# Attention scores by head, w_ada in pieces of 256 rows, and more buffers for the first shift and scale, in a two-block network on one core

## The chip, the cores and the metric

One Trainium2 chip, one core of it. The metric is the device time of one execution in microseconds. Before: 2873.4 us, the median of 3 runs (2872.57 to 2875.65).

## The reference

`reference()` runs two transformer blocks on 256 tokens of width 2048, in fp32. The first block has two layers, and the change lies in these. Cut to what matters:

```python
mod = c_act @ w_ada[l] + b_ada[l]                  # one row of 2048 by [2048, 6144]
shift, scale, gate = jnp.split(mod, 3, axis=-1)
h = rms_norm(x, norm_g[l]) * (1.0 + scale[:, None, :]) + shift[:, None, :]
u, z_s, q, k, v, z_a = jnp.split(h @ w_in[l], splits, axis=-1)   # 6 x 1024 columns
y_s = s5_mixer(u, ...) * jax.nn.silu(z_s)          # a scan over the tokens, then w_glu
# q, k get rotary positions; 8 heads, each with two score maps of 64 dimensions
# per block of 128 queries: softmax of both causal maps, then
w = p[:, :, 0] - lam * p[:, :, 1]
out = jnp.einsum('bhqk,bkhe->bqhe', w, vf)         # values of 128 dimensions a head
y_a = (rms_norm(out, sub_g) * (1.0 - lambda_init)) * jax.nn.silu(z_a)
y = jnp.concatenate([y_s, y_a], axis=-1) @ w_out[l]
x = x + gate[:, None, :] * y
```

The second block (another recurrent mixer, a second attention, a feed-forward net and an embedding) is untouched.

## The kernel before

**The large products.** Every weight matrix is streamed once from HBM in tiles of 256 rows by 512 columns (512 KB). `product` (L203) handles one tile: SP issues its load into a buffer of the pool `wraw` (4 buffers), ScalarE (ACT) rounds it to `whi` (L213), VectorE (DVE) subtracts to get `wlo` (L214), three buffers each, and TensorE (PE) runs three products, high by high, high by low and low by high, into PSUM tiles `acc`: 24 matmuls with a moving operand of 256 in the feature-major form (L221), 12 with 512 in the token-major form (L244 to L246). A `wraw` buffer comes free when DVE has read it.

**Order.** The program is written as one sequence with side threads. `gemm` (L178) steps three lanes of generators after each product (`rate` steps per product); the s5 chain, the s5 maps and attention are such generators. A scheduler that simulates the engines turns the whole into one instruction order per engine, by program order and by when data and buffers come free; on the chip each engine then keeps its order. Loads stand in SP's one queue in that order too. `issue_after` fixes an order on one engine, `after` adds a wait for another engine's instruction or for a load.

**The modulation rows.** `mod_block` (L343) computes 2048 columns of `mod`. For each of 16 k it loads two pieces of 128 rows by 1024 columns (512 KB each, L360) and issues four fp32 matmuls (L364), one for each group of 32 array columns, that write `mod_rows`, one PSUM bank that is held through all 16 k. Each fp32 matmul appears as two instructions, so one k has 8. `self.after(mm, dma)` makes the first of them wait for the second piece. The pieces lie in `wada`, two buffers; only for layer 0's shift and scale (`early`) does the first piece use `wraw`. `mod_norm` (L385) calls it for one half of shift and scale.

- `setup_first` (L296) and `modulated` (L392) run the two halves for layer 0 ahead of and between the first products (columns `u` of w_in); nothing of the network can start without the first half.
- `mod_side` (L416) runs layer 0's gate and both halves of layer 1, and in layer 1 the gate. `product` takes one step of it whenever `side_due` passes 1, which grows by `side_rate` a product: 0.42 in layer 0, 0.2 in layer 1 (L959). Before w_out the gate has to be there (L1029); what is left at the end is drained (L1084).

**Attention.** `diff_attention` (L830) is a generator in lane 0 that starts with the w_glu products and must end before the second half of w_out's rows (L1082). It runs 16 units, one for each head and block of 128 queries. `scores(u)` issues two products `da_s` (L843), one per map, each with 64 rows of the array and a PSUM bank of its own, from a pool of four banks (`aux`) that `mod_rows` and the transposes use too; DVE adds the causal mask and takes the maximum (L849), ACT takes the exponential (L853), POOL and DVE scale and subtract (L856, L857) into `da_p`. `weights(u)` transposes it (L865) and copies it to `da_wT`, `values(u)` multiplies by v (L878), and `gated` finishes two heads at a time. The three stages of neighbouring units overlap: in one step `scores(u)`, `weights(u-1)` and `values(u-2)` are written down, then a `yield`. `da_p`, `da_y` and `za` lie in `t2` (5 buffers of 512 columns), `da_wT` in `t1` (6 of 256).

Of the kernel before, what the change touches and what calls it, by code (L numbers as in the profile page):

```python
# [16 lines left out]
D = 2048  # L17
# [3 lines left out]
KB = 2  # L21


class Net:
# [318 lines left out]
    def mod_block(self, l, starts, dst, early=False):  # L343


        nc = self.nc
        asrow = not isinstance(dst, list)
        if asrow:
            bias = self.t2("mod_bias")
            for g in range(4):  # L350
                c0 = starts[g // 2] + g % 2 * 512
                nc.sync.dma_start(bias[32 * g:32 * g + 32, :], self.I["b_ada"][l, c0:c0 + 512].partition_broadcast(32))
        ps = self.bank("mod_rows")
        for k in range(16):
            raws = []
            for j, c0 in enumerate(starts):
                shared = early and j == 0
                raw = (self.wraw if shared else self.cf).tile([128, KB, 512], F32, tag="wraw" if shared else "wada", name="wada",
                                                              bufs=None if shared else 2)
                dma = nc.sync.dma_start(raw[:].rearrange("p j n -> p (j n)"), self.I["w_ada"][l, k * 128:(k + 1) * 128, c0:c0 + 1024])  # L360
                raws.append(raw)
            for g in range(4):
                o = slice(32 * g, 32 * g + 32)
                mm = nc.tensor.matmul(ps[o, :], self.v1["c"][:, k:k + 1].to_broadcast([128, 32]), raws[g // 2][:, g % 2, :], start=k == 0, stop=k == 15,  # L364
                                      tile_position=(0, 32 * g), skip_group_check=True)
                if g == 0:
                    self.after(mm, dma)
# [462 lines left out]
    def diff_attention(self, qT, kT, v, nlam, sg, zd, hs, ls):  # L830

        nc = self.nc
        scale = 64 ** -0.5
        units, pairs = {}, {}

        def scores(u):
            h, t = u // 2, u % 2
            n = 128 * (t + 1)
# [3 lines left out]
            def product(m):  # L842
                return nc.tensor.matmul(sps[m][:, :n], qT[64 * m:64 * m + 64, h, t * 128:t * 128 + 128],  # L843
                                        kT[64 * m:64 * m + 64, h, :n], start=True, stop=True)
            with self.tc.issue_after(product(1).ins):
                product(0)
            p = [p[:, m * 256:m * 256 + n] for m in range(2)]
            for m in range(2):
                nc.vector.tensor_tensor_reduce(p[m], sps[m][:, :n], self.tri[:, 256 - n:], 1.0, -3e38,  # L849
                                               ALU.add, ALU.max, mx[:, m:m + 1])  # L850
            nc.vector.tensor_scalar(mx[:, 0:2], mx[:, 0:2], -scale, None, op0=ALU.mult)
            for m in range(2):
                nc.scalar.activation(p[m], p[m], AF.Exp, bias=mx[:, m:m + 1], scale=scale, accum_out=mx[:, 2 + m:3 + m])  # L853
            rr = self.ty("da_r", 2)
            nc.vector.reciprocal(rr, mx[:, 2:4])
            nc.gpsimd.tensor_scalar(p[1], p[1], rr[:, 1:2], nlam[:, 0:1], op0=ALU.mult, op1=ALU.mult)  # L856
            nc.vector.scalar_tensor_tensor(p[0], p[0], rr[:, 0:1], p[1], op0=ALU.mult, op1=ALU.add)  # L857
            units[u] = p[0]

        def weights(u):  # L860
            t = u % 2
            n = 128 * (t + 1)
            tps = self.bank("da_w")
            for b in range(t + 1):
                nc.tensor.transpose(tps[:, b * 128:b * 128 + 128], units[u][:, b * 128:b * 128 + 128], self.ident[:])  # L865
            wT = self.t1("da_wT")
            nc.scalar.copy(wT[:, :n], tps[:, :n])
            units[u] = wT, tps

        def values(u):  # L870
            h, t = u // 2, u % 2
            wT, tps = units.pop(u)
            if u % 4 == 0:
                pairs[h // 2] = self.t2("da_y"), self.ty("da_ss", 4)
            yk, ss = pairs[h // 2]
            o = tps[:, 256:384]
            for b in range(t + 1):
                nc.tensor.matmul(o, wT[:, b * 128:b * 128 + 128], v[b][:, h * 128:h * 128 + 128], start=b == 0, stop=b == t)  # L878
            a = u % 4
            self.copy(yk[:, a * 128:a * 128 + 128], o)  # L880
            junk = self.th("da_j")
            nc.scalar.activation(junk[:], yk[:, a * 128:a * 128 + 128], AF.Square, accum_out=ss[:, a:a + 1])

        def gated(p):
            yk, ss = pairs.pop(p)
            r = self.ty("da_rs", 4)
            self.rsqrt(r, ss, 1.0 / 128, EPS, 4)
            y = yk[:].rearrange("p (a e) -> p a e", a=4)
            nc.gpsimd.tensor_mul(y, y, r.unsqueeze(2).to_broadcast([128, 4, 128]))
            za = self.t2("za")  # L890
            self.hold(nc.sync.dma_start(za[:], zd[p]))
            yield
            yield
            tps = self.bank("da_t")
            for a in range(4):
                nc.tensor.transpose(tps[:, a * 128:a * 128 + 128], yk[:, a * 128:a * 128 + 128], self.ident[:])
            nc.vector.scalar_tensor_tensor(za[:], tps[:], sg, za[:], op0=ALU.mult, op1=ALU.mult)
            for a in range(2):
                self.split(hs[2 * p + a], ls[2 * p + a], za[:, a * 256:a * 256 + 256])

        late = iter(())
        for u in range(16 + 3):
            if u < 16:
                scores(u)
            if 0 <= u - 1 < 16:
                weights(u - 1)
            if 0 <= u - 2 < 16:
                values(u - 2)
            next(late, None)
            if u >= 6 and (u - 6) % 4 == 0 or u == 18:  # L910
                late = gated((u - 6) // 4)
                next(late)
            yield
        for _ in late:
            pass


    def layer(self, l, xr, R, src, maps):
        nc, I = self.nc, self.I
# [15 lines left out]
        nlam = V("nlam", 1)  # L935
# [113 lines left out]
        ss = self.ty(f"xs{l}", 16)  # L1049
# [36 lines left out]
        n = 2 * l + 2  # L1086
# [1029 lines left out]
```

## Time and profile before

| | |
|---|---|
| Runs | 2872.57, 2873.4, 2875.65 us |
| Profiled execution | 2872.03 us |
| Its span, first to last instruction | 2870.2 us |
| Mean granted clock of TensorE in it | 0.983 |
| PE busy | 2755.9 us, 96% of the span |
| DVE, ACT, POOL busy | 1855.7, 1364.6, 407.9 us |
| Moved by DMA | 580.22 MB, mean 202 GB/s |

PE is TensorE's matmuls, PEld its weight loads, SP the queue that issues nearly all loads. "x24" is a count of instructions. In a timeline, neighbouring matmuls of one kind are merged into a row; since matmuls overlap, what a row costs PE is the distance to the start of the next row, not its length. In the table of stages the busy time of each engine stands with its count in brackets; the last three columns are the clock that the throttle granted TensorE (1.00 is 2.4 GHz, 0.50 is 1.2 GHz), the mean busy share of the 16 DMA engines, and what they moved. In a wait, the name behind the arrow is what ended it.

Layer 0 lies at about 0 to 700 us of the span (the first half of shift and scale to about 80 us, the columns `u` to 180, z to 300, q, k and v to 475, w_glu to 550, w_out to 690), layer 1 at 700 to 1203, and the second block behind it.

### The profile page before, as it was taken

Reading aid. Unit: us, or ns where it says so; the run is one execution under the profiler, and the core shown is the slowest. Engines: PE = TensorE matmul, PEld = TensorE weight load, DVE = VectorE, ACT = ScalarE, POOL = GpSimd, SP = SyncE. Lnnn points to the kernel's source line nnn. Section 1 sums busy time; section 2 is a strip of 40 time slices with the busy share of each in tenths; the row PEclk is TensorE's granted clock in tenths of the full one; section 3 lists DMA queues with packets and bytes.
Section 4 is the critical chain, followed back from the end, with each engine's and each line's share of the span. In section 5 each row is a group of like instructions: output and inputs, shape, how many; then the busy total and the mean of one; then the engine's idle time right before and its main releaser. Section 6 shows DMA issues by size and latency. Waiting matters only on the chain.

```text
span 2870.2 us, 53720 instructions
## 1 busy us (share of the span) xinstructions
PE 2755.9 (96%) x21378; PEld 2377.4 (83%) x21378; DVE 1855.7 (65%) x3323; ACT 1364.6 (48%) x2287; POOL 407.9 (14%) x561
## 2 busy tenths in 40 slices
PE   5799999998999999999999999999999999999998
PEld 2488777776997778799889888987999999988877
DVE  2367954667589557767777766665776667654455
ACT  2453454565434455544444444445555555544444
POOL 5300240243003302002121100010010101000000
PEclk8999999999999999999999999999999999999999
DMA  8878777675566655775434455466655555655565
GB/s 269 306 231 273 266 253 268 230 268 175 191 219 217 205 172 177 235 238 159 134 114 149 137 148 167 160 224 231 187 178 189 182 183 183 199 195 193 193 219 168
DMA packets 305637, 580.22 MB, mean 202 GB/s; under 512 B 32517, under 2 KB 70209, under 8 KB 303977
## 3 DMA queue, kind: packets, MB, share of 16 engines
q1 hardware_dynamic: 305065, 575.73, 62.2%
q8 instruction: 168, 2.75, 0.4%
q0 software_dynamic: 320, 1.05, 0.2%
q14 instruction: 84, 0.69, 0.1%
HBM read 555.70 MB, written 20.99 MB: 201 GB/s over the span
## 4 chain that ended last, share of the span: by engine, by line
PE 85%; DMA 6%; DVE 5%; ACT 1%; issue 1%; POOL 1%; SPq 0%; DVEq 0%; POOLq 0%; ACTq 0%
PE acc L221 44%; PE acc L245 10%; PE acc L244 10%; PE acc L246 9%; PE mod_rows L364 3%; DMA wada<-in_w_ada 3%; DMA wraw<-in_w_in 2%; DVE wlo L214 1%; PE da_s L843 1%; PE s5g L722 1%; ACT whi L213 1%; PE rw_in L1381 0%; PE rw_mt L1341 0%; PE rw_in L1372 0%; PE s5y L784 0%
## 5 line engine op out<-in xcount | busy, mean ns | idle before, releaser
L214 DVE TENSOR_TENSOR wlo<-wraw,whi 128x1024 fp32r<-128x1024 f32 x802 | 1003.9, 1253 | 718.9 <-ACT whi L213 705.1
L213 ACT CAST whi<-wraw 128x1024 fp32r<-128x1024 f32 x802 | 834.3, 1041 | 1035.7 <-PE acc L221 521.3
L221 PE MATMUL acc<-ufh,whi 128*128 128x256 f32 x1408 | 391.2, 284 | 3.3 <-ACT ufh L498 3.3
L221 PE MATMUL acc<-ufl,whi 128*128 128x256 f32 x1408 | 389.5, 284 | 0.0
L221 PE MATMUL acc<-ufh,wlo 128*128 128x256 f32 x1408 | 388.1, 284 | 0.0
L221 PEld LDWEIGHTS acc<-ufh,whi 128*128 128x128 f32 x1408 | 267.7, 193 | 4.0 <-ACT ufh L498 4.0
L221 PE MATMUL acc<-u2h,wlo 128*128 128x256 f32 x944 | 267.0, 289 | 4.1 <-DVE wlo L214 4.1
L221 PE MATMUL acc<-u2h,whi 128*128 128x256 f32 x944 | 266.9, 289 | 2.1 <-ACT u2h L498 2.1
L221 PEld LDWEIGHTS acc<-ufl,whi 128*128 128x128 f32 x1408 | 267.1, 193 | 0.0
L221 PEld LDWEIGHTS acc<-ufh,wlo 128*128 128x128 f32 x1408 | 266.2, 193 | 0.0
L221 PE MATMUL acc<-u2l,whi 128*128 128x256 f32 x944 | 263.8, 287 | 0.0
L221 PE MATMUL acc<-hh,whi 128*128 128x256 f32 x768 | 213.4, 290 | 6.2 <-ACT whi L213 5.1
L221 PE MATMUL acc<-hh,wlo 128*128 128x256 f32 x768 | 210.6, 287 | 1.5 <-DVE wlo L214 1.5
L221 PE MATMUL acc<-hl,whi 128*128 128x256 f32 x768 | 208.7, 284 | 1.6 <-DVE hl L494 1.6
L221 PEld LDWEIGHTS acc<-u2h,wlo 128*128 128x128 f32 x944 | 178.7, 192 | 7.7 <-DVE wlo L214 4.5
L221 PEld LDWEIGHTS acc<-u2h,whi 128*128 128x128 f32 x944 | 178.7, 192 | 5.7 <-ACT u2h L498 2.5
L221 PEld LDWEIGHTS acc<-u2l,whi 128*128 128x128 f32 x944 | 178.2, 192 | 2.0 <-issue 0.3
L221 PEld LDWEIGHTS acc<-hh,whi 128*128 128x128 f32 x768 | 144.8, 194 | 20.7 <-ACT whi L213 8.3
L364 PE MATMUL mod_rows<-wada,v 128*32 128x512 f32 x768 | 122.2, 655 | 37.4 <-DMA wada<-in_w_ada 33.8
L245 PE MATMUL acc<-wlo,hh 128*128 128x512 f32 x384 | 154.1, 401 | 2.8 <-DVE wlo L214 2.8
L221 PEld LDWEIGHTS acc<-hh,wlo 128*128 128x128 f32 x768 | 144.3, 194 | 9.9 <-issue 5.0
L246 PE MATMUL acc<-whi,hl 128*128 128x512 f32 x384 | 150.3, 391 | 0.0
(635 smaller groups left out, 5644.3 us busy)
## 6 DMA issues: line engine op xcount, KB each, us to landing
wraw<-in_w_in SPq DMA_DIRECT2D x288, 512.0 KB
wada<-in_w_ada SPq DMA_DIRECT2D x192, 512.0 KB
wraw<-in_w_up SPq DMA_DIRECT2D x176, 512.0 KB
wraw<-in_w_out SPq DMA_DIRECT2D x96, 512.0 KB
wraw<-in_w_down SPq DMA_DIRECT2D x88, 512.0 KB
wraw<-in_w_in SPq DMA_DIRECT2D x72, 256.0 KB
wraw<-in_w_glu SPq DMA_DIRECT2D x32, 512.0 KB
wraw<-in_w_ple_gate SPq DMA_DIRECT2D x28, 512.0 KB
```

The source lines that it names most:

```text
L213: nc.scalar.copy(hi[:, :nk, :nw], raw[:, :nk, :nw])
L214: nc.vector.tensor_sub(lo[:, :nk, :nw], raw[:, :nk, :nw], hi[:, :nk, :nw])
L221: return nc.tensor.matmul(o, w[:, i, fs[f]], x[k0 + i], start=first, stop=stop, skip_group_check=True)
L244: nc.tensor.matmul(o, xh[k][:, tsl], hi[:, i, :nw], start=st, stop=False)
L245: nc.tensor.matmul(o, xh[k][:, tsl], lo[:, i, :nw], start=False, stop=False)
L246: mm = nc.tensor.matmul(o, xl[k][:, tsl], hi[:, i, :nw], start=False, stop=sp)
L364: mm = nc.tensor.matmul(ps[o, :], self.v1["c"][:, k:k + 1].to_broadcast([128, 32]), raws[g // 2][:, g % 2, :], start=k == 0, stop=k == 15, ...
L722: nc.tensor.matmul(ps[n, p * 64:p * 64 + 64], wts[q][:, p, i, n], u4[:, P % 4, P // 4, :], start=True, stop=True, tile_position=(0, 64 * g))
L843: return nc.tensor.matmul(sps[m][:, :n], qT[64 * m:64 * m + 64, h, t * 128:t * 128 + 128], kT[64 * m:64 * m + 64, h, :n], start=True, stop ...
```

## The change

1. **Scores by heads.** `scores(h)` treats a head's two query blocks together: the four products go one after another (256-wide map 1, then map 0, then the 128-wide ones), the two blocks of one map share a PSUM bank. The first product waits for the last reduction of the head before, the 256-wide reductions wait for the head's last product of their map. The negation, the reciprocal, the copy of transposed weights and the copy of values are issued once per head. `weights` and `values` go by heads as well; `da_wT` moves from `t1` to `t2`, the 128-wide `da_p` from `t2` to `t1`. The loop has two yields per head: 21 in all, where there were 19.
2. **w_ada in pieces of 256 rows.** Outside `early`, a step takes two k: four loads, then 16 instructions, the first of which waits for the last load. The first k's pieces lie in `wada`, the second's in `wraw`. The side rates fall to 0.23 and 0.11.
3. **First half of the first shift and scale.** `early` is 2 there, 1 for the second half. With 2, the second piece of k with k % 8 above 1 goes to a buffer of `wlo` (even k) or `whi` (odd k).

```diff
@@ mod_block
-        for k in range(16):
+        nk = 1 if early else 2
+        for k0 in range(0, 16, nk):
             raws = []
-            for j, c0 in enumerate(starts):
-                shared = early and j == 0
-                raw = (self.wraw if shared else self.cf).tile([128, KB, 512], F32, tag="wraw" if shared else "wada", name="wada",
-                                                              bufs=None if shared else 2)
...
+            for k in range(k0, k0 + nk):
+                for j, c0 in enumerate(starts):
+                    if (j == 0 if early else k > k0):
+                        pool, tag = self.wraw, "wraw"
+                    elif early == 2 and k % 8 > 1:
+
+                        pool, tag = (self.whi, "whi") if k % 2 else (self.wlo, "wlo")
+                    else:
+                        pool, tag = self.cf, "wada"
+                    raw = pool.tile([128, KB, 512], F32, tag=tag, name="wada", bufs=2 if tag == "wada" else None)
...
+            for i in range(nk):
+                k = k0 + i
+                for g in range(4):
...
+                    if i == g == 0:
+                        self.after(mm, dma)
             yield
@@ mod_norm
-        yield from self.mod_block(l, [h * 1024, D + h * 1024], [self.shf[l][:, ks], self.scl[l][:, ks]], l == 0)
+        yield from self.mod_block(l, [h * 1024, D + h * 1024], [self.shf[l][:, ks], self.scl[l][:, ks]], (2 - h) * (l == 0))
@@ diff_attention
-        def scores(u):
-            h, t = u // 2, u % 2
...
-            with self.tc.issue_after(product(1).ins):
-                product(0)
...
+        def scores(h):
+
             sps = [self.bank("da_s") for _ in range(2)]
-            mx = self.ty("da_mx", 4)
-            p = self.t2("da_p")
...
+            mx = self.ty("da_mx", 8)
+            p = [self.t1("da_p0"), self.t2("da_p")]
+            at = lambda t: slice(128 * t, 128 + 256 * t)
+
+            def product(t, m):
+                return nc.tensor.matmul(sps[m][:, at(t)], qT[64 * m:64 * m + 64, h, t * 128:t * 128 + 128],
+                                        kT[64 * m:64 * m + 64, h, :128 * (t + 1)], start=True, stop=True)
+            first = product(1, 1)
+            if read:
+                self.after(first, read.pop())
+            last = [None, None]
+            with self.tc.issue_after(first.ins):
+                mm = product(1, 0)
+            for m in (1, 0):
+                with self.tc.issue_after(mm.ins):
+                    mm = last[m] = product(0, m)
+            for t in range(2):
+                n = 128 * (t + 1)
+                for m in range(2):
+                    red = nc.vector.tensor_tensor_reduce(p[t][:, m * n:m * n + n], sps[m][:, at(t)], self.tri[:, 256 - n:], 1.0, -3e38,
+                                                         ALU.add, ALU.max, mx[:, 2 * t + m:2 * t + m + 1])
+                    if t:
+                        self.after(red, last[m])
+            read.append(red)
...
+        def weights(h):
             tps = self.bank("da_w")
...
+            for i, (t, b) in enumerate(((0, 0), (1, 0), (1, 1))):
+                nc.tensor.transpose(tps[:, i * 128:i * 128 + 128], p[t][:, b * 128:b * 128 + 128], self.ident[:])
+            wT = self.t2("da_wT")
+            nc.scalar.copy(wT[:, :384], tps[:, :384])
...
-        for u in range(16 + 3):
...
+        for h in range(8 + 3):
+            if h < 8:
+                scores(h)
+            if 0 <= h - 1 < 8:
+                weights(h - 1)
+            if 0 <= h - 2 < 8:
+                values(h - 2)
             next(late, None)
-            if u >= 6 and (u - 6) % 4 == 0 or u == 18:
-                late = gated((u - 6) // 4)
+            if h >= 4 and h % 2 == 0:
+                late = gated(h // 2 - 2)
                 next(late)
             yield
+            if h < 10:
+                yield
@@ layer
-        self.side, self.side_rate = self.mod_side(l), 0.42 if l == 0 else 0.2
+        self.side, self.side_rate = self.mod_side(l), 0.23 if l == 0 else 0.11
```

## Rows read from the trace of the kernel before

**Rows 1.** The page, part 1: busy us, share of the span, instructions.

```profile
PE 2755.9 (96%) x21378; PEld 2377.4 (83%) x21378; DVE 1855.7 (65%) x3323; ACT 1364.6 (48%) x2287; POOL 407.9 (14%) x561
```

**Rows 2.** The page, part 4: the chain that ended last, by engine.

```profile
PE 85%; DMA 6%; DVE 5%; ACT 1%; issue 1%; POOL 1%; SPq 0%; DVEq 0%; POOLq 0%; ACTq 0%
```

**Rows 3.** Stages: length, busy us by engine, granted clock, DMA share, GB/s.

```profile
30.00:50.00 20.00, 11.96 (x74) 5.58 (x75) 4.87 (x21) 2.97 (x7) 17.32 (x60) 0.64 0.84 241
50.00:80.00 30.00, 18.01 (x116) 6.18 (x118) 4.90 (x13) 11.88 (x34) 19.94 (x43) 0.78 0.87 297
80.00:90.00 10.00, 8.32 (x70) 3.42 (x62) 5.28 (x11) 7.24 (x20) 4.39 (x7) 0.66 0.70 241
90.00:160.00 70.00, 55.73 (x446) 38.74 (x447) 31.15 (x57) 29.44 (x65) 13.79 (x21) 0.95 0.90 315
...
240.00:300.00 60.00, 58.41 (x473) 51.45 (x472) 55.31 (x167) 20.76 (x23) 0.00 (x0) 1.00 0.86 289
300.00:480.00 180.00, 177.11 (x996) 129.00 (x994) 113.36 (x212) 83.27 (x130) 52.40 (x60) 1.00 0.78 264
480.00:600.00 120.00, 117.27 (x721) 85.86 (x722) 71.46 (x208) 65.20 (x175) 25.80 (x31) 1.00 0.70 239
```

**Rows 4.** Timeline of PE, layers 0 and 1: start us, us, instruction.

```profile
563.84 0.49 PE L843 MATMUL da_s<-kT,qT 64*128 64x128 f32 x4
564.26 0.73 PE L246 MATMUL acc<-whi,ysl 128*128 128x512 f32 x2
...
569.94 1.06 PE L364 MATMUL mod_rows<-wada,v 128*32 128x512 f32 x8
570.93 0.50 PE L245 MATMUL acc<-wlo,ysh 128*128 128x512 f32 x1
...
577.36 0.39 PE L245 MATMUL acc<-wlo,ysh 128*128 128x512 f32 x1
577.58 0.39 PE L246 MATMUL acc<-whi,ysl 128*128 128x512 f32 x1
577.90 0.70 PE L843 MATMUL da_s<-kT,qT 64*128 64x256 f32 x2
578.53 0.50 PE L244 MATMUL acc<-whi,ysh 128*128 128x512 f32 x1
...
1117.57 0.70 PE L843 MATMUL da_s<-kT,qT 64*128 64x256 f32 x4
1118.20 0.73 PE L245 MATMUL acc<-wlo,ysh 128*128 128x512 f32 x2
```

**Rows 5.** Groups by line: count | busy us, mean ns | idle before.

```profile
L214 DVE TENSOR_TENSOR wlo<-wraw,whi 128x1024 fp32r<-128x1024 f32 x802 | 1003.9, 1253 | 718.9 <-ACT whi L213 705.1 <-issue 8.2 <-DMA wraw<-in_w_in 1.7
L213 ACT CAST whi<-wraw 128x1024 fp32r<-128x1024 f32 x802 | 834.3, 1041 | 1035.7 <-PE acc L221 521.3 <-PE acc L246 384.0 <-issue 53.3
...
L843 PE MATMUL da_s<-kT,qT 64*128 64x128 f32 (+1 forms) x128 | 30.1, 380 | 0.0
```

**Rows 6.** Stage of layer 0's attention, tile `da_s` alone.

```profile
480.00:612.00 132.00, 17.20 (x64) 8.48 (x64) 11.00 (x32) 1.00 0.72 244
```

**Rows 7.** Waits of PE, 160 to 660 us: total, times, longest.

```profile
PE mod_rows L364 <- DMA wada<-in_w_ada: 4.6, 6, 1.7
```

**Rows 8.** Waits of SP's queue, 160 to 660 us.

```profile
SPq L360 <- PE mod_rows L364: 84.9, 44, 5.1
```

**Rows 9.** The chain in order of time: start us, us, what.

```profile
370.80 8.45 DMA wada<-in_w_ada
...
847.09 14.59 PE acc L221 x120
```

**Rows 10.** Timeline of PE in layer 1's v product.

```profile
1022.20 1.04 PE L364 MATMUL mod_rows<-wada,v 128*32 128x512 f32 x2
```

**Rows 11.** Stages of layers 0 and 1, tile `mod_rows` alone.

```profile
160.00:700.00 540.00, 55.17 (x388) 8.59 (x392) 0.68 (x1) 1.17 (x2) 0.99 0.73 247
700.00:1205.00 505.00, 24.66 (x128) 3.31 (x120) 0.68 (x1) 0.00 (x0) 0.99 0.61 198
```

More of the change, by code (lines that the diff above doesn't have):

```diff
@@ L353, in mod_block @@
         ps = self.bank("mod_rows")
[L354 removed]
+        nk = 1 if early else 2
+        for k0 in range(0, 16, nk):
             raws = []
[L356 to L367 removed]
+            for k in range(k0, k0 + nk):
[7 more added lines that the diff above has]
+                    raw = pool.tile([128, KB, 512], F32, tag=tag, name="wada", bufs=2 if tag == "wada" else None)
+                    dma = nc.sync.dma_start(raw[:].rearrange("p j n -> p (j n)"), self.I["w_ada"][l, k * 128:(k + 1) * 128, c0:c0 + 1024])
+                    raws.append(raw)
+            for i in range(nk):
+                k = k0 + i
+                for g in range(4):
+                    o = slice(32 * g, 32 * g + 32)
+                    mm = nc.tensor.matmul(ps[o, :], self.v1["c"][:, k:k + 1].to_broadcast([128, 32]), raws[2 * i + g // 2][:, g % 2, :],
+                                          start=k == 0, stop=k == 15, tile_position=(0, 32 * g), skip_group_check=True)
+                    if i == g == 0:
+                        self.after(mm, dma)
             yield
@@ L834, in diff_attention @@
         units, pairs = {}, {}
-        def scores(u):
-            h, t = u // 2, u % 2
-            n = 128 * (t + 1)
+        read = []
+        def scores(h):
             sps = [self.bank("da_s") for _ in range(2)]
-            mx = self.ty("da_mx", 4)
-            p = self.t2("da_p")
-            def product(m):
-                return nc.tensor.matmul(sps[m][:, :n], qT[64 * m:64 * m + 64, h, t * 128:t * 128 + 128],
-                                        kT[64 * m:64 * m + 64, h, :n], start=True, stop=True)
-            with self.tc.issue_after(product(1).ins):
-                product(0)
[L847 to L858, printed above, removed]
@@ L860, in weights @@
-        def weights(u):
-            t = u % 2
-            n = 128 * (t + 1)
-            tps = self.bank("da_w")
[L864 to L873, printed above, removed]
+            mx = self.ty("da_mx", 8)
@@ new lines, in scores @@
+            read.append(red)
+            nc.vector.tensor_scalar(mx[:, 0:4], mx[:, 0:4], -scale, None, op0=ALU.mult)
+            for t in range(2):
+                n = 128 * (t + 1)
+                for m in range(2):
+                    i = 2 * t + m
+                    pm = p[t][:, m * n:m * n + n]
+                    nc.scalar.activation(pm, pm, AF.Exp, bias=mx[:, i:i + 1], scale=scale, accum_out=mx[:, 4 + i:5 + i])
+            rr = self.ty("da_r", 4)
+            nc.vector.reciprocal(rr, mx[:, 4:8])
@@ new lines, in scores @@
+            for t in range(2):
+                n = 128 * (t + 1)
+                p0, p1 = p[t][:, :n], p[t][:, n:2 * n]
+                nc.gpsimd.tensor_scalar(p1, p1, rr[:, 2 * t + 1:2 * t + 2], nlam[:, 0:1], op0=ALU.mult, op1=ALU.mult)
+                nc.vector.scalar_tensor_tensor(p0, p0, rr[:, 2 * t:2 * t + 1], p1, op0=ALU.mult, op1=ALU.add)
+            units[h] = p
+        def weights(h):
+            tps = self.bank("da_w")
+            p = units[h]
+            for i, (t, b) in enumerate(((0, 0), (1, 0), (1, 1))):
+                nc.tensor.transpose(tps[:, i * 128:i * 128 + 128], p[t][:, b * 128:b * 128 + 128], self.ident[:])
+            wT = self.t2("da_wT")
+            nc.scalar.copy(wT[:, :384], tps[:, :384])
+            units[h] = wT, tps
@@ L874, in values @@
+        def values(h):
+            wT, tps = units.pop(h)
+            if h % 2 == 0:
                 pairs[h // 2] = self.t2("da_y"), self.ty("da_ss", 4)
             yk, ss = pairs[h // 2]
[L876 to L881, printed above, removed]
@@ L882, in values @@
-            nc.scalar.activation(junk[:], yk[:, a * 128:a * 128 + 128], AF.Square, accum_out=ss[:, a:a + 1])
+            for t in range(2):
+                for b in range(t + 1):
+                    i = t + b
+                    nc.tensor.matmul(tps[:, t * 128:t * 128 + 128], wT[:, i * 128:i * 128 + 128], v[b][:, h * 128:h * 128 + 128],
+                                     start=b == 0, stop=b == t)
+            a = h % 2 * 2
+            self.copy(yk[:, a * 128:a * 128 + 256], tps[:, :256])
@@ L884, in gated @@
+            for t in range(2):
+                junk = self.th("da_j")
+                nc.scalar.activation(junk[:], yk[:, (a + t) * 128:(a + t) * 128 + 128], AF.Square, accum_out=ss[:, a + t:a + t + 1])
         def gated(p):
```

6 lines of the change are left out of this document (removed).

## The prediction

> **What bounds the kernel now.** I read the page first, then the chain, then the work by stages. The page [rows 1] gives TensorE (PE) 2755.9 of 2870.2 us busy and no other engine over 65%. The chain that ended last [rows 2] lies on PE for 85% and on DMA for 6%. So a microsecond counts where PE issues something else than the large products (`acc`), and where PE waits. The stages [rows 3] show two regimes. Up to 160 us PE has idle time (11.96 of 20 us busy, 18.01 of 30, 55.73 of 70) and the DMA engines are busy for 70 to 90%: loads set the pace, at 315 GB/s from 90 to 160 us but at 241 GB/s from 30 to 50 and from 80 to 90 us. Later PE is all but full (58.41 of 60, 177.11 of 180, 117.27 of 120 us). There, only PE's own work and its rare waits can be saved.
>
> The profiled execution took 2872.0 us (span 2870.2), 1.4 us under the median of 2873.4. The sum is made against 2872.0 and 1.4 is added at the end. A measurement of this kernel can tell about 0.2%, 5.7 us, from no change.
>
> **The scores, by heads.** Before, each of 16 units per layer issues two products, one in each half of the array's rows; the change issues four for a head, one after another. The number of products, transposes and value products stays; what can change is how far they overlap. The trace has both cases [rows 4]. At 563.84 the two products of a 128-query unit run together (x4: each fp32 product is two instructions) and PE goes on 0.42 us later. At 577.90 one 256-wide product runs alone (x2) and takes 0.63 us, and its partner takes the same again elsewhere. In layer 1 a 256-wide pair that stays together (x4) takes 0.63 us as well (1117.57 to 1118.20). A head with both pairs together costs 0.42 + 0.63 + 0.1 for the break in the stream = 1.15 us, 16 heads 18.4 us. The trace spends 30.1 us [rows 5], 17.20 of it in layer 0 [rows 6], where one of four small PSUM banks is held by `mod_rows` the whole time and the pairs fall apart. The new code asks that a head's first product follow the last reduction of the head before, so that both banks are free together. **Term: -12** (30.1 to 18.4). The wait has a price: all of PE's queue stands behind that product. A reduction is late by about one subtraction of the stream that gets ahead of it on DVE (L214, 1.25 us [rows 5]), 14 heads x 1.25 = 17 us at the worst; I take nothing, since today's products wait for the same reductions through the banks. The second wait, of the 256-wide reductions for the head's last product, delays DVE's queue by under 1 us, and whoever waits for `wlo` has two more converted tiles. **Bounds:** -13 without the break (16 x 1.05 = 16.8), 0 if the pairs stay apart as now, +17 with the waits.
>
> **Fewer breaks.** The `acc` matmul at 577.36 stands 0.22 us ahead of the next; the one at 577.58 stands 0.32 ahead of the burst that follows, and the first behind a burst lasts 0.50 (570.93, 578.53) where 0.39 is usual [rows 4]. Scores, transposes and values are 16 bursts each per layer, with split pairs some 110 in both layers; afterwards 48. Some 60 breaks at 0.1 us would be -6; some bursts stand back to back already. **Term: -4** (0 to -6). The saved instructions on DVE and ACT (negation, reciprocal, copies in half the number) are off the path, since DVE is 60% and ACT 54% busy from 480 to 600 us [rows 3].
>
> `da_wT` moves to the `t2` buffers. Two `da_y`, `za`, `da_p` and `da_wT` just fill five of them, so the next head's first reduction may wait for a buffer. A head has the time of two units to make up for it, with half as many hand-overs of banks, and PE is covered meanwhile by w_glu's products and the first half of w_out (117.27 of 120 us [rows 3]); I cost it at nothing. If attention ended 10 us later, PE would idle for up to that ahead of `yah`, in each layer.
>
> **w_ada in pieces of 256 rows.** A step of the side work has 8 instructions now (0.99 us from 569.94 to 570.93 [rows 4]) and 16 afterwards; gate 0, both halves of layer 1's norm and gate 1 are 64 such bursts, afterwards 32. Of each pair one break is saved, between the 0.1 us ahead of a burst and the 0.2 us that both its sides add: 32 x 0.16 = **-5** (bounds -3 and -6; splitting is a rival, below). PE waits for w_ada's landing 4.6 us, 6 times, between 160 and 660 us [rows 7], because two buffers hold only one step: SP waits 44 times for `mod_rows` [rows 8] and the load starts only then, at 370.80 us 8.45 us ahead of its landing [rows 9]. With a step every 4.3 products (1/0.23), 12.7 us at 2.92 us a product (120 steps in 14.59 us, 24 to a product [rows 9]), and the four loads spread over it, I take **-2** (bounds -4.6 and +5, should four loads land later than two).
>
> The price is in the weight stream. All 16 wait for the last of four loads. The second 128 rows take two of the four `wraw` buffers, and their DMAs stand in SP's queue ahead of the stream's, the z stores and x loads. What a piece waits for on SP (the release of a `wraw` buffer by DVE's `wlo`), all behind it wait for too. In a step, two `wraw` and three converted tiles are left, a lead of 5 x 2.92 = 14.6 us, less ACT's 1.04 and DVE's 1.25 us [rows 5] twice, about 10 us, for a landing of 8.45 us [rows 9]. So it should just hold; ACT's long waits for PE at L213 [rows 5] say that the stream is ahead today. From 240 to 300 us DVE is busy 55.31 of 60 us and DMA 0.86 [rows 3]: there I expect misses of 1.5 us at four steps. **Term: +6** (0 to 48, which is 1.5 us at all 32).
>
> **The first half of the first shift and scale.** Its second pieces go round two buffers, now eight. The first pieces still have four, so the loads can run four steps ahead instead of two. What the low-rate stretches hold [rows 3]: 30 to 50 us at 241 instead of 315 GB/s is 20 x (1 - 241/315) = 4.7 us, 50 to 80 us at 297 is 1.7, 80 to 90 us at 241 is 2.3, but that one is the hand-over to the products. PE there runs at a mean granted clock of 0.64, that is partly at 1.2 GHz, with its transposes between the rows, so not all of it comes back. **Term: -4** (bounds: -8.7; +3, if the small loads that the s5 maps wait for now queue behind w_ada).
>
> The Trainium skill, "DMA: Bandwidth & Descriptors", Specifications, gives about 358 GB/s as what HBM leaves one core. By that the stretches of 241 and 297 GB/s would hold 11.6 us rather than 6.4, an estimate from that page, and the sum would be some 5 us lower. The trace speaks against it: over 70 us with loads always queued it shows 315 GB/s.
>
> **Sum:** -12 - 4 - 5 - 2 - 4 + 6 = -21; 2872.0 - 21 = 2851.0, as a median 2852.
>
> **Rivals.**
> *Slower: the stream starves.* With w_ada in half of `wraw`, the lead of 10 us falls under the landing time at every step, and PE stands before `acc` waiting for `wlo`. It decides once four queued loads and a stream tile take over 10 us. For it: 8.45 us today with less queued, DMA busy 0.78 to 0.86 from 240 to 480 us. Against: the waits of L213 for PE. Price 48, less the gains of 27: about 2893. Chance 0.18.
> *No change: split bursts.* In layer 1, where a step comes every 5 products and so its data lie ready early, single groups of two instructions stand between products [rows 10]: 1.04 us for a quarter of the work. Layer 1 spends 24.66 us on 128 instructions, 0.193 each, layer 0 55.17 on 388, 0.142 each [rows 11]. If the rarer steps bring layer 0 there, 384 x 0.051 = 20 us are lost: 2871. The whole bursts of layer 0's feature-major stretches speak against it. Chance 0.14.
> *The change doesn't do what it says:* the pairs still part for want of a bank, and the 12 us don't come: 2864. Chance 0.08.
>
> **The numbers.** My forecast has 0.60. Its own range is 2836 to 2866. The range of 2832 to 2884 adds the split bursts, the parted pairs and the mild part of starvation; what lies out is its worse part and a sum of all good ends (2829). Faster: 0.58 + 0.06 of parted pairs + 0.03 = 0.67; same 0.12; slower 0.17 of starvation + 0.04 = 0.21.
>
> **What would show it.** Right: `da_s` under 20 us in bursts of 8, `mod_rows` in bursts of 16 and near 0.13 us per instruction from 160 us on, the hand-over at 160 us some 4 us earlier, PE still full. Wrong: PE waits for `wlo` or `whi` in hundreds of ns after each w_ada step (starvation), x2 bursts of `mod_rows` in layer 0 (splitting), x2 or x4 bursts of `da_s` (parted), or an idle PE ahead of `yah` in either layer (attention late).

## The result, and the profile after

| | before | after |
|---|---|---|
| Runs, median | 2873.0 us (2871.2 to 2875.7, 4 runs) | 2842.4 us (2841.1 to 2847.7, 4 runs) |
| Ratio, 95% interval | | 0.989 (0.9877 to 0.9904) |
| Profiled execution, its span | 2872.03, 2870.2 us | 2842.31, 2840.3 us |

The change takes 30.6 us off; 21 were forecast (2852, range 2832 to 2884). The page after, part 1 and the first line of part 4, answering to [rows 1] and [rows 2]:

```profile
PE 2727.8 (96%) x21378; PEld 2379.3 (84%) x21378; DVE 1839.1 (65%) x3283; ACT 1358.0 (48%) x2263; POOL 402.9 (14%) x561
...
PE 80%; DMA 8%; DVE 7%; ACT 2%; POOL 1%; issue 1%; SPq 1%; DVEq 0%; ACTq 0%; POOLq 0%
```

PE has the same 21378 instructions and 28.1 us less of busy time; of the 29.9 us of the span, all but 1.8 are, on balance, PE's own work. Yet the chain lies less on PE (80% for 85%) and more on DMA and DVE: something was won and something else moved closer to the end. The stages after, as in [rows 3]:

```profile
30.00:50.00 20.00, 7.73 (x37) 1.85 (x37) 3.52 (x19) 0.81 (x3) 18.36 (x64) 0.58 0.92 304
50.00:80.00 30.00, 22.46 (x188) 11.20 (x184) 10.55 (x24) 16.53 (x46) 19.23 (x40) 0.83 0.87 291
80.00:90.00 10.00, 8.86 (x91) 6.19 (x90) 8.74 (x17) 9.35 (x26) 7.88 (x9) 1.00 0.97 340
90.00:160.00 70.00, 56.46 (x424) 41.61 (x423) 30.12 (x57) 27.96 (x56) 13.60 (x20) 0.88 0.79 275
240.00:300.00 60.00, 57.31 (x451) 49.16 (x450) 52.20 (x162) 19.79 (x21) 0.00 (x0) 1.00 0.85 297
...
480.00:600.00 120.00, 118.43 (x836) 94.90 (x838) 77.32 (x213) 75.53 (x208) 38.90 (x49) 1.00 0.73 251
```

From 30 to 50 us DMA moves 304 GB/s where it moved 241, and from 80 to 90 us 340 for 241; from 50 to 80 us nothing changes (291 for 297), and from 90 to 160 us it moves less, 275 for 315. The first `acc` starts 8.9 us earlier (at 81.0 for 89.9 us), the last copy of `uT` 5.8. Up to that copy both kernels have moved 49.6 MB. Between 240 and 300 us PE is 1.1 us less busy than before. The tiles `da_s` (first two rows) and `mod_rows` (last two) alone, as in [rows 6] and [rows 11]:

```profile
400.00:700.00 300.00, 10.84 (x64) 6.91 (x64) 9.91 (x32) 0.98 0.69 235
900.00:1205.00 305.00, 11.16 (x64) 6.39 (x64) 9.89 (x32) 0.99 0.64 211
...
160.00:700.00 540.00, 49.24 (x384) 10.51 (x384) 0.69 (x1) 1.16 (x2) 0.99 0.72 247
700.00:1205.00 505.00, 16.42 (x128) 3.44 (x128) 0.68 (x1) 0.00 (x0) 0.99 0.65 213
```

`da_s` goes from 30.1 to 22.0 us, `mod_rows` from 0.142 and 0.193 us per instruction to 0.128 in both layers. PE's timeline in layer 0 shows both forms that a head takes:

```profile
483.38 0.28 PE L221 MATMUL acc<-gl,whi 128*128 128x256 f32 x1
483.50 0.28 PE L221 MATMUL acc<-gh,wlo 128*128 128x256 f32 x1
483.71 0.92 PE L855 MATMUL da_s<-kT,qT 64*128 64x256 f32 x8
484.57 1.92 PE L374 MATMUL mod_rows<-wada,v 128*32 128x512 f32 x16
486.42 0.39 PE L221 MATMUL acc<-gh,whi 128*128 128x256 f32 x1
486.64 0.28 PE L221 MATMUL acc<-gl,whi 128*128 128x256 f32 x1
...
498.41 0.70 PE L855 MATMUL da_s<-kT,qT 64*128 64x256 f32 x2
499.03 0.39 PE L221 MATMUL acc<-gl,whi 128*128 128x256 f32 x1
```

At 483.71 a whole head goes in one burst of 8 and takes 0.86 us to the next burst, 0.94 with the 0.09 us more that the `acc` matmul ahead of it takes. At 498.41 one 256-wide product goes alone (x2, 0.62 us), and the other six instructions follow later. Six of 16 heads stay whole, three in each layer; all scores together are 28 bursts, where they were 49.

Where the time went is read from three marks that each kernel has: the last copy of `uT` (columns `u` done), the last copy of `v`, and the last sum `xo` of each layer's w_out (shown for both layers of before and after). Their rows in before, after and the run `heads_alone` (below); the two times behind the colon are the starts of the first and the last one:

```profile
L96 ACT COPY uT<-acc x2: 578/579/580, 177.8 to 180.7; 128x512 f32<-128x512 f32 x2
L98 DVE COPY v<-acc x2: 691/691/691, 449.9 to 475.3; 128x512 f32<-128x512 f32 x2
L1074 DVE TENSOR_TENSOR xo<-xo,xold x8: 681/693/1277, 615.8 to 689.1; 128x512 f32<-128x512 f32 x8
L1074 DVE TENSOR_TENSOR xo<-xo,xold x8: 679/688/693, 1153.3 to 1205.7; 128x512 f32<-128x512 f32 x8
```

```profile
L96 ACT COPY uT<-acc x2: 582/582/583, 172.0 to 174.9; 128x512 f32<-128x512 f32 x2
L98 DVE COPY v<-acc x2: 686/689/692, 454.7 to 477.0; 128x512 f32<-128x512 f32 x2
L1107 DVE TENSOR_TENSOR xo<-xo,xold x8: 682/688/770, 603.8 to 675.4; 128x512 f32<-128x512 f32 x8
L1107 DVE TENSOR_TENSOR xo<-xo,xold x8: 680/684/693, 1118.3 to 1178.4; 128x512 f32<-128x512 f32 x8
```

```profile
L96 ACT COPY uT<-acc x2: 579/581/583, 182.3 to 185.2; 128x512 f32<-128x512 f32 x2
L98 DVE COPY v<-acc x2: 692/692/692, 454.2 to 479.6; 128x512 f32<-128x512 f32 x2
L1097 DVE TENSOR_TENSOR xo<-xo,xold x8: 680/694/1084, 602.0 to 679.4; 128x512 f32<-128x512 f32 x8
```

The differences of such marks (us), with four runs that come below:

| | before | after | heads_alone | heads_and_early | pieces_256_layer1 | rows256_alone | unmerged_128 |
|---|---|---|---|---|---|---|---|
| to the end of `u` | 180.7 | 174.9 | 185.2 | 173.4 | 175.1 | 183.8 | 178.0 |
| z, q, k, v of layer 0 | 294.6 | 302.1 | 294.4 | 293.5 | 294.6 | 304.7 | 306.6 |
| w_glu, attention, w_out of layer 0 | 213.8 | 198.4 | 199.8 | 200.0 | 199.9 | 213.9 | 192.5 |
| layer 1 | 516.6 | 503.0 | 507.8 | 510.1 | 501.1 | 508.7 | 503.9 |
| the rest | 1664.5 | 1661.9 | 1665.1 | 1660.9 | 1665.3 | 1662.2 | 1660.9 |

After wins 5.8 us in the first stage, 15.4 under layer 0's attention and 13.6 in layer 1, and **loses 7.5 us** between `u` and `v`. The rest, whose source is the same in all kernels, differs by about 5 us between the thirteen profiled executions of this case (1661 to 1666), so a few us between single stages of two executions show nothing by themselves.

### The profile page after: what moved, and what is told of

It is laid out like the page before. It is cut to its first block, busy times and chain, and to the rows that moved or that the text cites. A ratio compares the mean times of both kernels' runs of the same rounds, so it can differ in the third digit from the quotient of the medians.

```text
span 2840.3 us, 53566 instructions
## 1 busy us (share of the span) xinstructions
PE 2727.8 (96%) x21378; PEld 2379.3 (84%) x21378; DVE 1839.1 (65%) x3283; ACT 1358.0 (48%) x2263; POOL 402.9 (14%) x561
## 3 DMA queue, kind: packets, MB, share of 16 engines
q0 software_dynamic: 320, 1.05, 0.1%
## 4 chain that ended last, share of the span: by engine, by line
PE 80%; DMA 8%; DVE 7%; ACT 2%; POOL 1%; issue 1%; SPq 1%; DVEq 0%; ACTq 0%; POOLq 0%
PE acc L221 44%; PE acc L245 8%; PE acc L244 8%; PE acc L246 8%; DMA wraw<-in_w_in 3%; DVE wlo L214 3%; PE mod_rows L374 2%; DMA wraw<-in_w_out 1%; ACT whi L213 1%; DMA wada<-in_w_ada 1%; PE da_s L855 1%; PE s5g L732 1%; DVE s5m L742 1%; DVE X L745 0%; DVE s5m L744 0%
## 5 line engine op out<-in xcount | busy, mean ns | idle before, releaser
L221 PEld LDWEIGHTS acc<-u2l,whi 128*128 128x128 f32 x944 | 178.0, 192 | 2.0 <-issue 0.3
L221 PEld LDWEIGHTS acc<-hl,whi 128*128 128x128 f32 x768 | 145.7, 195 | 3.7 <-DVE hl L504 2.9
```

Of the source, the lines that this page charges most:

```text
L221: return nc.tensor.matmul(o, w[:, i, fs[f]], x[k0 + i], start=first, stop=stop, skip_group_check=True)
```

## The experiments

Each was timed against the kernel before on its own chip (2874.8 to 2877.2 us there), so ratios are compared. Their intervals are about 0.0015 to either side. The forecast's parts stand as theory; the rivals are that parts hide each other, or that the gain has another mechanism than the one named.

| | median us (range) | ratio |
|---|---|---|
| after | 2842.4 (2841.1 to 2847.7) | 0.9890 |
| heads_alone | 2852.2 (2849.8 to 2855.6) | 0.9921 |
| rows256_alone | 2869.9 (2866.7 to 2881.3) | 0.9988 |
| early_alone | 2863.7 (2862.8 to 2865.1) | 0.9961 |
| unmerged_128 | 2845.0 (2843.1 to 2847.8) | 0.9897 |
| heads_and_early | 2841.4 (2839.6 to 2842.1) | 0.9881 |
| heads_and_256 | 2853.9 (2848.0 to 2857.2) | 0.9921 |
| no_hand_over | 2841.4 (2836.7 to 2844.6) | 0.9879 |
| halves_apart | 2839.4 (2838.1 to 2841.8) | 0.9874 |
| one_half_of_rows | 2848.5 (2839.3 to 2851.4) | 0.9894 |
| pieces_256_layer1 | 2835.1 (2832.2 to 2837.8) | 0.9855 |
| layer1_halves_no_wait | 2832.7 (2829.2 to 2835.1) | 0.9846 |

**One part alone.** `heads_alone` is before with the new `diff_attention`, `rows256_alone` before with `nk = 2` and the new side rates, `early_alone` before with the buffers of `early == 2`:

```diff
 heads_alone:    - def scores(u):              + def scores(h):     (with weights, values and the loop)
 rows256_alone:  - 0.42 if l == 0 else 0.2     + 0.23 if l == 0 else 0.11      + nk = 1 if early else 2
 early_alone:    - ..., l == 0)                + ..., (2 - h) * (l == 0))      + nk = 1
```

> The kernel before with the scores by heads and nothing else of the change (w_ada by 128 rows, old side rates, old buffers for the first half). Additive parts: the scores' tile takes 20 us of PE instead of 30, the breaks some 2 to 3 us less, attention in layer 0 ends some 30 us earlier; in all -10 us (2861 to 2865 where before is 2873). Rival, that the gain is one of the three parts together or of a new instruction order as a whole: within 4 us of the kernel before, or over 16 us faster.

> The kernel before with w_ada in pieces of 256 rows and the new side rates alone. Additive parts: PE's mod_rows after 160 us falls from 79 to about 66 us (pairs in bursts of 16, no bursts of 2), a few us come back as waits for wlo in layer 0's q product; in all -11 us (2859 to 2865). Rival, that the pieces pay only with the shorter attention, or that the stream starves without it: within 4 us of before or slower.

> The kernel before with the added buffers for layer 0's first half of shift and scale alone. Additive: the last product of the columns u ends at 175 instead of 181 us, everything behind it shifts: -6 us (2865 to 2869). Rival, that the first 160 us are bound by the bytes or that what is gained is lost by layer 0's end: within 2 us of before.

Measured: -22.6, -4.9 and -11.0 us. Together that would be -38.5; the change has -30.6. The stage table puts the heads' gain where it belongs: 14.0 us under layer 0's attention and 8.8 in layer 1, and nothing ahead of it. There the instruction order of all five engines is the same as before up to about the first score product, and yet the end of `u` came 4.5 us later in this execution (185.2 for 180.7; `rows256_alone`, with the same order in that stage, has 183.8): so much the first stage differs from run to run. Its `da_s`, two stages, and those waits of PE before (475 to 1205 us) that get shorter or go:

```profile
400.00:700.00 300.00, 9.46 (x64) 6.35 (x64) 9.60 (x32) 0.98 0.74 251
900.00:1205.00 305.00, 10.95 (x64) 6.39 (x64) 9.72 (x32) 0.99 0.62 202
```

```profile
PE spread L481 <- DVE diag L480: 7.4, 1, 7.4
...
PE acc L246 <- DVE ysl L102: 2.3, 3, 1.1
...
PE da_w L865 <- DVE da_p L857: 1.4, 1, 1.4
```

Scores give 9.7 us of busy time. The two stages together give 22.8 us. Added up by the distances from each PE instruction's start to the next, with idle time of over 0.4 us kept apart, that is 8.1 us less in steps that begin with `da_s`; 7.4 less in steps of `acc`, which has as many instructions as before, but is broken off by attention's bursts 53 times instead of 86; 4.6 less of idle time (the waits for `ysl` and `da_w` are gone, the one for `diag` is 5.7 for 7.4 us); and 1.6 in `mod_rows`. The last 1.1 us are spread.

`rows256_alone` shows why w_ada's part is worth little by itself. Its `mod_rows`, stages as in [rows 11]:

```profile
160.00:700.00 540.00, 57.15 (x384) 11.07 (x384) 0.68 (x1) 1.15 (x2) 0.99 0.72 243
700.00:1205.00 505.00, 16.42 (x128) 3.44 (x128) 0.68 (x1) 0.00 (x0) 0.98 0.61 201
```

Layer 1 saves its 8 us, layer 0 none: among attention's units its bursts of 16 are cut up (57.15 us for 384, 0.149 each, no less than before). And from `u` to `v` it takes 304.7 us, 10.1 more than before; what lies behind that is taken up below.

**Bursts or buffers?** `unmerged_128` is after with one k a step again, where the pieces of every second k still take `wraw`:

```diff
-        nk = 1 if early else 2
+        nk = 1
-                    if (j == 0 if early else k > k0):
+                    if (j == 0 if early else k % 2):
-  0.23 if l == 0 else 0.11
+  0.46 if l == 0 else 0.22
```

> The kernel after, but a step of the side work takes one k again (pieces of 128 rows, side rates 0.46 and 0.22), with the pieces of odd k in wraw, so that two steps can be loaded ahead as before the merge. If the merge of bursts is what pays: PE's breaks come back, 32 x 0.2 = +6 us against the kernel after (2848), or +12 where bursts split as before. If the second pair of buffers is what pays (loads ahead, no wait for landing): within 3 us of the kernel after (2842).

2845.0 us, 0.9897 [0.9882, 0.9913]: the merged bursts themselves are worth 2.6 us by the medians, no more than the intervals can tell. Its marks:

```profile
L96 ACT COPY uT<-acc x2: 579/581/583, 175.1 to 178.0; 128x512 f32<-128x512 f32 x2
L98 DVE COPY v<-acc x2: 682/686/691, 456.0 to 484.6; 128x512 f32<-128x512 f32 x2
L1107 DVE TENSOR_TENSOR xo<-xo,xold x8: 679/688/1054, 606.8 to 677.1; 128x512 f32<-128x512 f32 x8
L1107 DVE TENSOR_TENSOR xo<-xo,xold x8: 679/684/694, 1120.9 to 1181.0; 128x512 f32<-128x512 f32 x8
```

By them it is slow and fast where after is: 499.1 us from `u` to the end of layer 0 (after 500.5, `heads_and_early` 493.5) and 503.9 in layer 1 (503.0 and 510.1). So, as far as one execution can show it, both the loss in layer 0 and the gain in layer 1 come mainly with the pieces in `wraw`, that is with loads further ahead and a shared pool, and not with the merged bursts.

**Two parts together.**

```diff
 heads_and_early (after, and):   -        nk = 1 if early else 2     +        nk = 1
                                 -  0.23 if l == 0 else 0.11         +  0.42 if l == 0 else 0.2
 heads_and_256   (after, and):   -  (2 - h) * (l == 0))              +  l == 0)
```

> The change without its second part: one k of w_ada per step, pieces in the two wada buffers only, rates 0.42 and 0.2; scores by heads and the added buffers for the first shift and scale stay. Theory A, the parts are worth here what they are worth alone: 2874.8 - 22.6 - 11.0 = 2841, at or under the full change's 2842.4 and mod_rows near 58 us from 160 to 700 us as in the heads run alone; then 256-row pieces add nothing in company. Rival B, the w_ada part pays only once attention by heads leaves the bank and PE's order to it (alone it cost 12 us in layer 0 up to q and won 8 us of mod_rows in layer 1): 2848 to 2852, 6 to 10 us over the full change, lost mostly in mod_rows.

> The change without its third part: the first shift and scale has its old buffers. Theory A, the early buffers are worth what they are worth alone: 2842.4 + 11 = 2853, with the end of columns u some 6 us later than with the full change and 5 us more lost behind. Rival B, only the 6 us of the first stage count and the rest of the 11 was the order of layer 0 that the scheduler happened to write: 2848. Rival C, parts overlap since the head form alone showed a first stage 5 us longer: 2842 to 2845.

`heads_and_early` comes out at 0.9881, after at 0.9890: **w_ada's part adds nothing**, as theory A had it, and -22.6 - 11.0 = -33.6 is what these two give together. `heads_and_256` is at 0.9921, 8.9 us over after by the ratios (11.5 by medians of two chips): within the intervals, the early buffers are worth in company what they are worth alone. In four profiles without these buffers (before and three of the runs) the last `uT` copy starts at 181, 184, 185 and 186 us, in nine with them between 173 and 178.

What eats w_ada's gain shows between `u` and `v` (302.1 us for 293.5). The chain of after (first line) and of `heads_and_early` from 175 to 480 us:

```profile
by line: DMA wraw<-in_w_in 15.4%; PE acc L221 13.8%; PE acc L245 9.8%; DVE wlo L214 9.6%; PE acc L244 9.4%; PE acc L246 9.2%; PE mod_rows L374 6.8%; ACT whi L213 3.1%; PE s5y L794 2.9%; PE s5g L732 2.9%; DVE X L745 2.8%; DVE s5m L744 2.7%; 
```

```profile
by line: PE acc L221 28.1%; PE acc L244 13.7%; PE acc L245 13.4%; PE acc L246 12.9%; PE mod_rows L374 10.4%; DMA wada<-in_w_ada 8.9%; PE s5g L732 2.9%; PE s5y L794 2.7%; PE s5y L788 1.2%; PE toT L837 1.1%; DVE wlo L214 0.8%; PE s5f L805 0.7
```

With w_ada in `wraw`, the chain of this stretch goes through the landing of w_in's tiles and their conversion; without it, through PE. PE's and SP's waits after, 160 to 480 us (total, times, longest), and last PE's only one in `heads_and_early`:

```profile
PE acc L245 <- DVE wlo L214: 3.8, 4, 1.6
PE acc L221 <- DVE wlo L214: 1.3, 2, 0.8
PE acc L244 <- ACT whi L213: 1.0, 1, 1.0
...
SPq L367 <- DVE wlo L214: 28.2, 14, 3.8
...
PE mod_rows L374 <- DMA wada<-in_w_ada: 3.7, 4, 1.8
```

w_ada's loads (L367) stand 14 times in SP's queue until DVE has freed a `wraw` buffer, with the stream's loads behind them; PE then waits 6.1 us for `wlo` and `whi`, where without w_ada's part it waits 3.7 us, for `mod_rows`' data alone (before as well, [rows 7]). So the waits are not the whole of the 8.6 us. By the distances between PE's instructions, 3.1 of them are more idle time (in pieces of over 0.4 us), 2.6 are 24 `mod_rows` instructions that `heads_and_early` does later, 1.7 are longer steps of `acc`, and the rest is spread. The loss is not one of a single execution: from `u` to the end of layer 0 the six profiles with scores by heads and w_ada's pieces in `wraw` in layer 0 take 496.6 to 501.8 us, the four with scores by heads and without such pieces 492.1 to 494.5.

**256 rows where the stream has slack.** If that is the cause, the larger steps should pay in layer 1, where DMA is busy 0.61 to 0.65 of the time, without the loss in layer 0:

```diff
-        nk = 1 if early else 2
+        nk = 2 if l == 1 and starts[0] == 2 * D else 1
-  0.23 if l == 0 else 0.11
+  0.42 if l == 0 else 0.11
```

> The full change with steps of 256 rows only for layer 1's gate (side rate 0.11 there); everything that runs in layer 0 takes 128 rows a step at rate 0.42 as before. Theory A, read from the stages of the full change beside the run without w_ada's part: in layer 0 the steps of 256 rows cost 9 us from the end of u to the end of v (PE waits for wlo and whi, and more steps there) and give 1.5 back under attention, in layer 1 they win 6.5 us. Then this is 2841.4 - 5 = 2836, with no wait of PE for wlo between 160 and 480 us and mod_rows near 58 us in layer 0 and 13.5 us for 104 instructions in layer 1. Rival B, the bursts are moved about and their breaks are not on the path: 2841 as both.

2835.1 us, 0.9855 [0.9841, 0.9868], faster than after. In the table of marks the stretch from `u` to `v` is back at 294.6 us and layer 1 at 501.1. PE's only wait for weights from 160 to 480 us and its `mod_rows`:

```profile
PE mod_rows L374 <- DMA wada<-in_w_ada: 2.5, 3, 1.7
...
160.00:700.00 540.00, 54.40 (x384) 8.25 (x384) 0.68 (x1) 1.17 (x2) 0.99 0.75 249
700.00:1205.00 505.00, 17.46 (x128) 3.58 (x128) 0.68 (x1) 0.00 (x0) 0.99 0.65 213
```

No wait for `wlo` is left, and layer 1's instructions cost 0.136 us where [rows 11] had 0.193. (24 more of them run in layer 1 than expected.) Rival B is out. The run doesn't part the larger steps from the loads further ahead, since layer 1 has both; by `unmerged_128` it is mainly the second that pays.

**What holds a head's four products together, and what that is worth.** `one_half_of_rows` leaves out the scores of map 0.

```diff
 no_hand_over (after, and):   -            if read:
                              -                self.after(first, read.pop())
 halves_apart (after, and):   -            for m in (1, 0):
                              +            for t, m in ((0, 1), (1, 0), (0, 0)):
 one_half_of_rows (after, and):   - qT[64 * m:64 * m + 64, ...], kT[64 * m:64 * m + 64, ...]
                                  + qT[64:128, ...],             kT[64:128, ...]
```

> The full change without the wait of a head's first product for the last reduction of the head before. Theory A, that wait keeps a head's four products together: without it heads split more often than now (now 3 of 8 whole in layer 0, 4 of 8 in layer 1), da_s rises from 22 us toward 26 and the time by 4 to 6 us, to about 2847. Rival B, the written order on PE and the two banks do that by themselves and the wait is always over before: 2842, da_s 22 us. Rival C, the wait holds PE's queue up: 2836 to 2840, da_s unchanged.

> The full change with a head's products in the order map 1 256 wide, map 1 128 wide, map 0 256 wide, map 0 128 wide, so that neighbours mostly use the same half of the array's rows and only one of three seams lies between the halves. Theory A, the gain of the head form is the overlap of the two halves: 0.63 + 0.42 us a head are not hidden any more, 16 heads x 0.5 to 1.05 = 8 to 17 us, so 2850 to 2859, with da_s at 30 to 38 us. Rival B, the gain is the shorter attention (half the hand-overs, w_out no longer held up), whatever the products cost: da_s 30 us and more as before the change, but the time within 4 us of the full change's 2842.

> The full change, but map 0's score products read map 1's rows of q and k, so that all four products of a head lie in the same half of the array's rows; the scores of map 0 are left out. It takes the overlap of the two halves away, which the order alone did not (there a head still took 0.94 us, as in the written order). Theory A, overlap is what the head form buys: per head 0.63 + 0.42 us come back, 16 heads x 1.05 = 17 us, less what was lost to split heads already: da_s near 36 us and the time 12 to 17 us over 2842.4, 2854 to 2859. Rival B, the head form's gain is fewer breaks and fewer waits, and the products' own time is half hidden: da_s up by as much, but the time under 2850.

Without the hand-over wait: 0.9879, `da_s` 22.7 us: rival B, the wait does nothing that can be measured. `halves_apart` missed its aim. Its whole heads (first row) take as long as after's, and a map's two products alone (second row, x4) as long as both maps together; `one_half_of_rows` (below) did take the overlap away:

```profile
482.00 0.93 PE L855 MATMUL da_s<-kT,qT 64*128 64x256 f32 x8
...
496.23 0.92 PE L855 MATMUL da_s<-kT,qT 64*128 64x256 f32 x4
```

```profile
483.92 1.57 PE L855 MATMUL da_s<-kT,qT 64*128 64x256 f32 x8
485.42 1.06 PE L374 MATMUL mod_rows<-wada,v 128*32 128x512 f32 x8
...
400.00:700.00 300.00, 13.90 (x64) 9.72 (x64) 9.95 (x32) 0.98 0.69 236
900.00:1205.00 305.00, 14.43 (x64) 9.56 (x64) 9.91 (x32) 0.98 0.64 210
```

A head in one half takes 1.50 us to the next burst where both halves take 0.86: overlap saves 0.64 us a whole head, not the 1.05 that theory A put on it, since products that follow one another in a burst cost less than products in bursts of their own. `da_s` rises by 6.3 us to 28.3. The time rises by 6 us in the medians but hardly in the ratio (0.9894 for 0.9890), with runs from 2839 to 2851; it stays under rival B's 2850, and how much of the 6.3 us reaches the end stays open. Its profiled execution has the same instruction order as after's on every engine; there the two stages with scores are 7.8 us longer (201.1 and 508.1 us), but it is the slowest of the five runs.

**The best so far.** `pieces_256_layer1` with the order of `halves_apart` and without the wait:

> The run before this one, with the order of the run with halves apart and without the hand-over wait: the three edits that each came out at or under the full change. If they add: 2836 - 3 - 1 = 2832, with da_s at 19 us. If the 3 us of the order were a chance of the profile: as the run before this one, 2836.

2832.7 us, 0.9846 [0.9832, 0.9859], 44.5 us under the kernel before on its chip. The time is as the sum had it, but the intervals of this run and the one before overlap, and `da_s` is 23.3 us, not 19: the order of the products is not what the 2.5 us come from, if they are real.

## Why the prediction was right, and where its sizes were off

The direction, the bound (PE's own instructions, the loads in the first stage) and the main mechanisms held. By its own steps:

- **Scores -12** (30.1 to 18.4): 8.1 measured (22.0). A whole head is cheaper than the 1.15 us forecast, 0.94, but ten of 16 heads still part, in layer 0 as a first product alone and six instructions behind it. The price of the hand-over wait, taken as nothing, was nothing (`no_hand_over`); the second wait, of the 256-wide reductions, was not tested.
- **Fewer breaks -4**: this is one of the two terms that were mis-sized. With `heads_alone` at -22.6 and scores at 8 to 9.7, some 13 us are left, 7.4 of them in the steps of `acc` (-4, with -6 as the bound) and 4.6 in idle time that the forecast costed at nothing. The number of breaks saved was put too high and the price of one too low: scores, transposes and values went from 113 bursts to 73, not to 48, but a break costs the `acc` instruction ahead of it 0.09 us (483.50 to 483.71, where 0.12 is usual) and the one behind it 0.10 (486.42 to 486.64), about 0.2 for the forecast's 0.1. For the 33 breaks that `heads_alone` saves this is 6.6 us, an estimate from these rows, of the 7.4. Fewer bursts of scores (49 to 28) also mean fewer hand-overs: layer 0's scores run from 480 to 537 us, before from 489 to 591, DVE waits for `da_s` 6 times (6.3 us in all) instead of 29 times (32.1), and PE's waits for `ysl` are gone. Attention late ahead of `yah` was listed as a wrong sign; it went the other way.
- **w_ada -5 and -2, against +6 for the stream**: the net forecast of -1 was right within the intervals (`heads_and_early` is 1 us under after by the medians, 2.6 by the ratios), each side was larger. `mod_rows` gives 14.2 us of busy time from 160 us on (79.83 to 65.66 by [rows 11] and the rows above), 8.2 of them in layer 1, where split bursts all but end; the forecast had splitting only as a rival's threat. Most of that end comes without the merge (`unmerged_128`: 18.04 us for 120 instructions there, 0.150 each). Beside `heads_and_early`, by distances from the end of `u` to the end of layer 1, `mod_rows` costs 9.7 us less and all else 9.5 more. Of the 8.6 us from `u` to `v`, 6.0 are left without the work that only lies elsewhere. The mechanism is the one named: loads of w_ada wait on SP for `wraw`, those of the stream behind them.
- **Early buffers -4**: 11 measured alone, 8.9 in company by the ratios; the other mis-sized term. The gaps of 30 to 50 and 80 to 90 us did fill. The step that failed is "not all of it comes back": it took the rates of one profile and half of what they hold, 8.7 us, and that profile was the quickest of four first stages (181 to 186 us); with the buffers they end about 9 us earlier, at 173 to 178.
- **The sum**: -22.6 - 11 + 1 = -32.6 by the experiments (the 1 is after over `heads_and_early`), -30.6 measured, -21 forecast. The head form (scores and breaks, -16 for -22.6) and the early buffers (-4 for -11) were each some 7 us too small; the result still lies in the forecast's own range (2836 to 2866). The sum of all good ends, given as 2829, is 2835 by the bounds that the prediction states.
- **Rivals.** The stream starved in its mild form alone: 6.1 us of waits, not at every step. Split bursts did not come with the larger steps in company (0.128 us each in layer 0), but did in `rows256_alone`. Pairs that part did come, in ten heads, and cost about 4 of the 12 us; that it was for want of a bank, no run shows.

## What to carry to other kernels

A buffer pool that feeds the main stream is dear to share: side loads in the stream's pool cost some 5 us net in layer 0, where DMA is busier, and won some 6 us in layer 1, where the stream had slack; test such a change by stage before it is made for all. Interrupting a full stream of products has a price beside the interrupting work (here about 0.2 us each time), and each hand-over to another engine can add a wait: count bursts and hand-overs as well as instructions. And before a stage's gain is read from one profile, compare that stage over several executions of the same order; here the first one differed by 4.5 us.

## What the runs showed that was not expected

Products in different halves of the array's rows overlap though they are not neighbours. In `halves_apart` the program issues both products of map 1 and then both of map 0. In the whole head at 482.00 the second instruction to start, 13 ns after map 1's first, is read as map 0's, ahead of map 1's next: the rows don't name the half, but products of one half never start so close (in `one_half_of_rows` they start 0.11 to 0.32 us apart). The head takes no longer than with alternating maps, where a pair starts 6 ns apart. That tiles of the array work independently and in parallel is what the Trainium skill says ("TensorEngine Tiling (Array Packing)", Tiling Modes); the trace agrees and shows that it holds across four instructions of the program's order.

The loads reach 340 GB/s for the 10 us from 80 to 90 us, where the best such stretch up to 160 us before was 327 GB/s (90 to 100 us). So the 315 GB/s that the prediction took for full loading are not the most that this kernel can reach for 10 us.
